# Four projection matmuls drawn in front of a class-side score step instead of between its matmuls

## The chip, the cores and the metric

The kernel runs on one core of one Trainium2 chip. The metric is the device time of one execution in microseconds. Before the change it is 1135.92 us, the median of three runs (1135.29 to 1136.38).

## What is computed

One decoder layer with 1024 positions and width 1024, in float32. The normalised input goes through one projection; a quarter of its width feeds a pooling mixer, three quarters feed twelve attention heads of 64 channels. Each head is evaluated under three windowed patterns, and the three results are merged by their softmax denominators. Then come the output projection and a gated feed-forward part, each with a norm and a residual.

```python
DILATED_CONFIGS = ((128, 1), (512, 4), (2048, 16))
...
def reference(x, ...):
    h = rms_norm(x, ln_pre_mix[l])
    proj = h @ w_in[l]
    q, k = rope(q, pos), rope(k, pos)
    pool_out = multi_scale_pool(u_pool, w_pool[l], pool_scale[l])
    attn_out = dilated_attention(q, k, v).reshape(B, S, ATTN_WIDTH)
    mix = jnp.concatenate([pool_out, attn_out], axis=-1) @ w_out[l]
    x = x + rms_norm(mix, ln_post_mix[l])
    h = rms_norm(x, ln_pre_ffn[l])
    f = (jax.nn.silu(h @ w_gate[l]) * (h @ w_up[l])) @ w_down[l]
    x = x + rms_norm(f, ln_post_ffn[l])
```

## The kernel before, in words

**Units.** The heads are worked on in six pairs, and the positions in two halves h of 512. A pair and a half make a unit, twelve in all (0 to 11; `units`). Units 0, 2, 4, 6, 8 and 9 have h = 0, the others h = 1. Each unit has scores, a merge of the softmax terms, weights, turns (transposes of the weighted scores) and products with v.

**The scores.** `scores` (L802) makes eight steps of a unit: two heads `hd`, two sides, two steps `jj` each. Side 1 is the class side: positions with the same remainder by 4 are taken together, which serves the two dilated patterns. Side 0 is the natural side, positions in a row. A step takes one bank of PSUM (tag `s`, two banks that are used in turn) and makes four matmuls in it, two query blocks j times two parts n of q (`qh` high and `ql` low, which together hold float32 precision). q is the stationary operand, loaded into TensorE ahead of its matmul, and k the moving one. At the class side a query block is `q[n][:, hd, j::4]` (L823), at the natural side a run of 128 columns. At h = 0 a class block has 128 moving columns, at h = 1 it has 256 (`narrow`). VectorE then reduces each block with its mask (L846) and ScalarE exponentiates it (L849).

**The list of projections.** The projections of later units run between the attention steps, as a list of small steps (`Fill`, L679). A step of `proj_half` (L702) is one matmul of 512 columns, a step of `v_rows` (L738) two matmuls of 256 columns, and a step of `pool_proj` (L1010) one of 256; at the end of the attention a list of output projections takes over, with 512 columns. `pull` (L697) runs the next step of the current list, or nothing if the list is at its end. A plan, sorted by written positions (`emit`, L1080), sets which step comes when; slots of the list (`by`, L693) run it up to a given step, so that a step that has been pulled already isn't run again.

**Waiting.** `await_` (L659) keeps a planned clock. It pulls from the list until the clock has come to the due time of what the next step needs, for a score step the release of its bank (`("s", 0)`), and then makes a number of further pulls from a table. A pull counts 0.235 us on this clock, and the matmuls of a score step 0.47 us.

**Order.** All matmuls and transposes are kept in program order on TensorE (`mm`, L346), so that the order of the Python calls is that of the engine. At the class side the loop over n pulls once ahead of each of the four score matmuls (L831 to L834). In the profile a matmul is TensorE's PE, its weight load PEld; the tiles are `ps_s` for scores, `ps_pj` for most projections, `ps_t` for turns and `ps_o` for products.

Of the kernel before, what the change touches and what calls it, by code (L numbers as in the profile page):

```python
# [335 lines left out]
def view(ap, offset, dims):  # L336

    return bass.AP(tensor=ap.tensor, offset=ap.offset + offset, ap=[list(ap.ap[0])] + [list(d) for d in dims])
# [3 lines left out]
def hybrid_block(ctx: ExitStack, tc: tile.TileContext, xT, w_in, w_v, w_pin, w_pool, w_out, w_gate, w_up, w_down,  # L342
# [3 lines left out]
    def mm(*a, **k):  # L346
        return tc.keep_in_program_order(nc.tensor.matmul(*a, **k))  # L347
# [9 lines left out]
    def did(key):  # L357
        seen[key] = seen.get(key, 0) + 1

    def need(key, n):  # L360
        assert seen.get(key, 0) >= n, (key, n, seen.get(key, 0))
# [8 lines left out]
    def bank(tag):  # L370
        return psum.tile([P, 512], F32, name="ps_" + tag, tag=tag)
# [254 lines left out]
    def by_class(ap):  # L626

        return ap.rearrange("p (c r) -> p r c", c=4)
# [30 lines left out]
    def await_(*keys, step=None):  # L659

        at = max([due.get(k, 0.0) for k in keys] or [0.0])
        more, n = G["x"].get(step, 0), 0
        while clock[0] < at + min(0, more) * 0.235 and n < G["fl"]:
            f = Fill.now
            if f is None or f.n >= len(f.steps):
                break
            pull()
            n += 1
        for n in range(more):
            pull()  # L670
# [26 lines left out]
    def pull():  # L697
        f = Fill.now
        if f is not None and f.n < len(f.steps):
            f.upto(f.n + 1)  # L700
# [98 lines left out]
    def narrow(side, h, j):  # L799
        return h == 0 and (side == 1 or j == 0)  # L800

    def scores(pr, h):  # L802

        un = pr.un[h] = Pair()
        un.sx = small.tile([P, 2, 2, 4, 2, 2], F32, name="sx", tag="sx", bufs=2)
        un.pp = {}

        def step(hd, side, jj):
            did(("s", pr.p, h))
            for i in range(h + 1):  # L810
                need(("k", pr.p, i), pr.p > 0)
            if jj == 0:
                un.pp[hd, side] = att.tile([P, 4, 256], F32, name="pp", tag="pp", bufs=PPB)
            pt = un.pp[hd, side]
            sx = un.sx
            q, kc = pr.q[h], pr.k
            await_(("s", 0), step=(unit_of[pr.p, h], "s", 4 * hd + 2 * (1 - side) + jj))
            s = bank("s")
            for j in (2 * jj, 2 * jj + 1):
                qb = 4 * h + j  # L820
                nb = 1 if narrow(side, h, j) else 2
                so = s[:, (j % 2) * 256:(j % 2) * 256 + nb * P]
                qs = slice(j * P, (j + 1) * P) if side == 0 else slice(j, 512, 4)  # L823
                kk = kc[:, hd]
                if side:
                    rhs = kk.rearrange("p (h c r) -> p h c r", h=2, c=4)[:, :nb, j]
                else:

                    b = qb + 1 - nb
                    rhs = view(kk, b // 4 * 512 + b % 4 * 32, [[P, 4]] + ([[32 + (b % 4 == 3) * 384, 2]] if nb == 2 else []) + [[1, 32]])  # L830
                for n in range(2):  # L831
                    if side:
                        pull()
                    mm(so, q[n][:, hd, qs], rhs, start=(n == 0), stop=(n == 1))  # L834
            clock[0] += 0.47
            due["s", 0], due["s", 1] = due.get(("s", 1), 0.0), clock[0] + G["ls"]
            due["m", pr.p, h] = clock[0] + G["lm"]
            for j in (2 * jj, 2 * jj + 1):
                nb = 1 if narrow(side, h, j) else 2
                lo = 256 - nb * P  # L840
                so = s[:, (j % 2) * 256:(j % 2) * 256 + nb * P]
                row, mask = pt[:, j, lo:], (mB if side else mA)[:, lo:]
                if side == 0:
                    so = by_class(so)
                    row, mask = (x.rearrange("p (r c) -> p r c", c=4) for x in (row, mask))
                nc.vector.tensor_tensor_reduce(  # L846
                    row, so, mask, op0=ALU.add, op1=ALU.min, scale=-0.125,
                    scalar=3e38, accum_out=sx[:, 0, side, j, hd, 0:1])
                nc.scalar.activation(pt[:, j, lo:], pt[:, j, lo:], AF.Exp,  # L849
                                     bias=sx[:, 0, side, j, hd, 0:1], scale=-1.0,  # L850
                                     accum_out=sx[:, 0, side, j, hd, 1:2])
        return [lambda a=a: step(*a) for a in [(hd, sd, jj) for hd in range(2) for sd in (1, 0) for jj in range(2)]]

    def merge(pr, h):
# [1114 lines left out]
```

## Time and profile before

| | us |
|---|---|
| median of three runs | 1135.92 |
| lowest and highest | 1135.29, 1136.38 |
| the profiled execution's own time | 1135.46 |
| its span on the core | 1133.6 |
| TensorE matmuls busy | 1125.0 |
| TensorE weight loads busy | 978.1 |
| VectorE busy | 782.1 |
| GpSimd busy | 587.1 |
| ScalarE busy | 563.8 |

The profile shows one execution. A row of the time line has the start in us from the beginning of the span, the duration in us, the engine, the line, the operation, the tiles (out<-in), the size of the array that is used, the shape (partitions x elements) and how many alike were merged (x1 is a single one). Matmuls are pipelined, so one starts before its predecessor's row has ended: the distance between the starts of two rows, not the duration, says what a matmul costs. A row of a group has the busy time in us, the mean in ns and, behind the bar, the idle time ahead. A row of waits has who waited for whom, the sum in us, the number of waits and the longest.

### The profile page before, as it was taken

The numbers are of one execution on the slowest core, as the hardware profiler recorded it, in microseconds if no ns is written. First come the engines' busy times: TensorE is split into PE (matmuls) and PEld (weight loads), VectorE is DVE, ScalarE is ACT, GpSimd is POOL, SyncE is SP. The second block draws the span as 40 slices with busy tenths as digits, with TensorE's granted clock in tenths as the row PEclk, the third lists the DMA queues.
The fourth block names the chain that finished last, engine by engine and source line by source line (L and its number), as shares of the span: only waits on it lengthen the run. The fifth ranks groups of instructions, "written<-read, shape, count | busy, mean of one in ns | idle before, by whom it ended". The sixth has DMA issues, their size and how long they took to land.

```text
span 1133.6 us, 17084 instructions
## 1 busy us (share of the span) xinstructions
PE 1125.0 (99%) x6076; PEld 978.1 (86%) x6076; DVE 782.1 (69%) x1455; ACT 563.8 (50%) x1092; POOL 587.1 (52%) x497
## 2 busy tenths in 40 slices
PE   9999999999999999999999999999999999999997
PEld 7999999999899888888788888888888888888897
DVE  7966879787987666979566755676566375464594
ACT  7356676776777765856323322322232436344430
POOL 0103645363576023242678655977586977665631
PEclk9999999999999999999999999999999999999999
DMA  8324151515137467430344344535454869766642
GB/s 285 118 80 168 57 168 41 183 57 167 58 112 263 168 221 276 151 112 28 140 167 176 148 158 160 204 139 204 168 185 168 278 207 369 247 198 195 204 167 75
DMA packets 85366, 189.04 MB, mean 167 GB/s; under 512 B 8736, under 2 KB 23584, under 8 KB 83872
## 3 DMA queue, kind: packets, MB, share of 16 engines
q1 hardware_dynamic: 84992, 187.68, 47.7%
q8 instruction: 48, 0.79, 0.3%
q14 instruction: 38, 0.31, 0.1%
q10 hardware_dynamic: 288, 0.27, 0.1%
HBM read 134.96 MB, written 52.95 MB: 166 GB/s over the span
## 4 chain that ended last, share of the span: by engine, by line
PE 93%; DMA 2%; POOL 2%; issue 1%; DVE 1%; SPq 0%; ACT 0%; DVEq 0%; POOLq 0%; ACTq 0%
PE ps_pj L347 34%; PE ps_s L347 24%; PE ps_o L347 23%; PE ps_t L347 8%; PE ps_t L350 3%; DMA wraw<-in_w_v_dram 1%; POOL whl L1561 1%; POOL fw L1561 1%; DMA rw<-in_w_up_dram 1%; DMA wraw<-in_w_in_dram 0%; DVE sq L510 0%; DMA ls<-in_lsel_dram 0%; PE ps_o L350 0%; POOL y L1762 0%; SPq L494 0%
## 5 line engine op out<-in xcount | busy, mean ns | idle before, releaser
L347 PE MATMUL ps_pj<-x,whl 128*128 128x512 f32 x480 | 141.8, 408 | 0.0
L1561 POOL TENSOR_TENSOR fw<-rw,fw 128x512 fp32r<-128x512 f32 x74 | 100.5, 1383 | 62.0 <-ACT fw L1559 62.0
L347 PE MATMUL ps_o<-tT,fw 128*128 128x512 f32 x504 | 117.8, 389 | 0.7 <-DVE p L1596 0.7
L907 POOL TENSOR_SCALAR pp<-pp,wv 128x256 f32<-128x256 f32 (+1 forms) x111 | 53.3, 502 | 115.8 <-ACT u L1025 45.6
L347 PEld LDWEIGHTS ps_o<-tT,fw 128*128 128x128 f32 x504 | 94.5, 188 | 20.7 <-DVE p L1596 1.1
L402 POOL TENSOR_TENSOR whl<-wraw,whl 128x512 fp32r<-128x512 f32 x52 | 68.9, 1347 | 73.8 <-ACT whl L398 71.8
L849 ACT ACTIVATE pp<-pp,sx 128x128 f32<-128x128 f32 (+1 forms) x192 | 89.4, 467 | 27.6 <-DVE sx L846 26.9
L1561 POOL TENSOR_TENSOR whl<-rw,whl 128x512 fp32r<-128x512 f32 x42 | 61.9, 1498 | 62.9 <-ACT whl L1559 62.9
L347 PEld LDWEIGHTS ps_pj<-x,whl 128*128 128x128 f32 x480 | 84.1, 189 | 9.1
L1559 ACT ACTIVATE fw<-rw 128x1024 fp32r<-128x1024 f32 x37 | 38.6, 1057 | 100.5 <-DVE rw L1527 45.2
L347 PE MATMUL ps_pj<-whl,x 128*128 128x256 f32 x528 | 81.4, 289 | 0.0
L1708 POOL TENSOR_TENSOR op<-rw,op 128x512 fp32r<-128x512 f32 x38 | 60.5, 1591 | 37.5 <-ACT op L1707 34.8
L1707 ACT ACTIVATE op<-rw 128x1024 fp32r<-128x1024 f32 x38 | 40.2, 1060 | 67.2 <-PE ps_t L347 32.7
L347 PEld LDWEIGHTS ps_pj<-whl,x 128*128 128x128 f32 x528 | 70.0, 192 | 0.2
L621 POOL TENSOR_TENSOR rsw<-rsw,sinr 128x512 f32<-128x512 f32 x20 | 26.8, 1339 | 81.3 <-DVE rsw L619 81.3
L955 DVE TENSOR_TENSOR ptr<-ps_t,ptr 128x512 fp32r<-128x512 f32 (+1 forms) x84 | 56.0, 667 | 17.8 <-ACT ptr L954 17.1
L954 ACT ACTIVATE ptr<-ps_t 128x512 fp32r<-128x512 f32 (+1 forms) x84 | 48.2, 574 | 28.7 <-PE ps_t L350 27.5
L347 PE MATMUL ps_pj<-b,fw 128*128 128x512 f32 x264 | 61.6, 389 | 0.0
L347 PEld LDWEIGHTS ps_pj<-b,fw 128*128 128x128 f32 x264 | 49.6, 188 | 10.3
L347 PE MATMUL ps_o<-ptr,v 128*128 128x128 f32 (+1 forms) x472 | 55.7, 254 | 0.0
L347 PEld LDWEIGHTS ps_o<-ptr,v 128*128 128x128 f32 x472 | 52.3, 163 | 3.2 <-DVE mix L921 0.3
L347 PE MATMUL ps_s<-k,qh 128*128 128x128 f32 (+1 forms) x192 | 54.4, 295 | 0.0
(322 smaller groups left out, 2921.5 us busy)
## 6 DMA issues: line engine op xcount, KB each, us to landing
rw<-bd SPq DMA_DIRECT2D x77, 256.0 KB, 4.9
v<-vd SPq DMA_DIRECT2D x22, 512.0 KB, 4.3
rw<-wsd SPq DMA_DIRECT2D x44, 256.0 KB, 4.0
rw<-in_w_gate_dram SPq DMA_DIRECT2D x20, 512.0 KB, 3.8
rw<-in_w_up_dram SPq DMA_DIRECT2D x20, 512.0 KB, 4.8
bd<-p SPq DMA_DIRECT2D x33, 256.0 KB, 2.7
rw<-in_w_down_dram SPq DMA_DIRECT2D x33, 256.0 KB, 4.7
fw<-in_w_down_dram SPq DMA_DIRECT2D x16, 512.0 KB, 4.0
```

The costliest lines, as they stand in the source:

```text
L347: return tc.keep_in_program_order(nc.tensor.matmul(*a, **k))
L350: return tc.keep_in_program_order(nc.tensor.transpose(dst, src, by))
L402: parts.append(eng.tensor_tensor(dst[:, 1, at:at + w], src[:, at:at + w], dst[:, 0, at:at + w].bitcast(F32), ALU.subtract))
L621: pin(eng[0].tensor_tensor(s, s, sinr[:, sl], ALU.mult))
L849: nc.scalar.activation(pt[:, j, lo:], pt[:, j, lo:], AF.Exp, bias=sx[:, 0, side, j, hd, 0:1], scale=-1.0, accum_out=sx[:, 0, side, j, hd, ...
L907: nc.gpsimd.tensor_scalar(pv, pv, un.wv[:, side, j, hd:hd + 1], 1.0, op0=ALU.mult, op1=ALU.mult)
L954: nc.scalar.activation(ptr[:, 0, :w], t[:, :w], AF.Copy)
L955: nc.vector.tensor_tensor(ptr[:, 1, :w], t[:, :w], ptr[:, 0, :w].bitcast(F32), ALU.subtract)
L1559: nc.scalar.activation(w[n][:, :, 0], raw[n], AF.Copy)
L1561: low[0] = nc.gpsimd.tensor_tensor(w[n][:, i, 1], raw[n][:, i], w[n][:, i, 0].bitcast(F32), ALU.subtract)
L1707: nc.scalar.activation(w[:, :, 0], raw, AF.Copy)
L1708: nc.gpsimd.tensor_tensor(w[:, 0, 1], raw[:, 0], w[:, 0, 0].bitcast(F32), ALU.subtract)
```

## The change

At the class side the step's four pulls are made at once, ahead of the step's `await_`. The pull ahead of each score matmul is gone, so that the four score matmuls are issued one after the other. At the natural side (side 0) `range(4 * side)` is empty, and nothing changes.

```diff
             sx = un.sx
             q, kc = pr.q[h], pr.k
+            for n in range(4 * side):
+                pull()
             await_(("s", 0), step=(unit_of[pr.p, h], "s", 4 * hd + 2 * (1 - side) + jj))
             s = bank("s")
             for j in (2 * jj, 2 * jj + 1):
...
                 for n in range(2):
-                    if side:
-                        pull()
                     mm(so, q[n][:, hd, qs], rhs, start=(n == 0), stop=(n == 1))
```

## The prediction

> **What bounds the kernel now.** I read the page first (busy shares, then the chain that ended last), then TensorE's own waits, then the groups of its weight loads, then the time line of TensorE around the steps that the diff touches.
>
> ```profile
> span 1133.6 us, 17084 instructions
> ...
> PE 1125.0 (99%) x6076; PEld 978.1 (86%) x6076; DVE 782.1 (69%) x1455; ACT 563.8 (50%) x1092; POOL 587.1 (52%) x497
> ```
>
> ```profile
> PE ps_o L347 <- DVE warm L454: 1.5, 1, 1.5
> PE ps_o L347 <- DVE p L1596: 0.7, 1, 0.7
> ```
>
> TensorE is busy 99% of the span, and the waits that it has on other engines add up to about 2 us, and both rows lie outside the attention units (the warm-up ahead of them, the feed-forward half behind). So there is no slack on TensorE into which longer work could go: what the score steps cost more or less on TensorE comes out at the end almost one to one. A busy 99% does not say that the stream runs at its best rate, though. A matmul has a weight load in front of it, and the question is which of the two sets the distance to the next matmul.
>
> ```profile
> L347 PEld LDWEIGHTS ps_pj<-x,whl 128*128 128x128 f32 x480 | 84.1, 189 | 9.1
> ...
> L347 PEld LDWEIGHTS ps_s<-k,ql 128*128 128x128 f32 x192 | 48.1, 251 | 1.1
> ```
>
> Both loads have the same shape, 128x128, but the load for a score takes 251 ns in the mean against 189 ns for one of a projection. Half of the score loads are class side. There q is read at every fourth column (`qs = slice(j, 512, 4)`, L823); the natural half reads it in a row. The class loads are the long ones, as the time line shows:
>
> ```profile
> 272.88 0.31 PEld L347 LDWEIGHTS ps_s<-k,ql 128*128 128x128 f32 x1
> 273.09 0.33 PEld L347 LDWEIGHTS ps_s<-k,qh 128*128 128x128 f32 x1
> 273.33 0.33 PEld L347 LDWEIGHTS ps_s<-k,ql 128*128 128x128 f32 x1
> ```
>
> They last 0.31 to 0.33 us and begin 0.21 and 0.24 us after one another.
>
> **The change, part by part.** The edit adds no instruction and takes none away. It moves four pulls (each one step of the running list of projection matmuls) from between the four class scores to the front of the step, ahead of its `await_`. No DMA is tied to the scores; a projection's first pull issues its weight DMA (SP) and split (ScalarE, GpSimd or VectorE), its last pull hands the result to the rope on VectorE, GpSimd and ScalarE; these now stand ahead of the step's score reductions and exponentials instead of between them. I cost that at nothing: it is less than one step earlier, and the busiest of these engines is at 69% (rival 3 is the case without that cover).
>
> *Interleaved, as it is now, 256 columns* (units with h = 1; unit 7's second class step):
>
> ```profile
> 275.54 0.40 PE L347 MATMUL ps_pj<-x,whl 128*128 128x512 f32 x1
> 275.77 0.28 PE L347 MATMUL ps_s<-k,qh 128*128 128x256 f32 x1
> ...
> 276.95 0.40 PE L347 MATMUL ps_pj<-x,whl 128*128 128x512 f32 x1
> ```
>
> The four pulls and four scores between the first and the last row take 276.95 - 275.54 = 1.41 us.
>
> *Following each other.* Unit 7's first class step had an exhausted list, so its four scores already stand together behind projections: exactly the new pattern.
>
> ```profile
> 272.64 0.40 PE L347 MATMUL ps_pj<-x,whl 128*128 128x512 f32 x1
> 272.88 0.28 PE L347 MATMUL ps_s<-k,qh 128*128 128x256 f32 x1
> ...
> 273.70 0.40 PE L347 MATMUL ps_pj<-x,whl 128*128 128x512 f32 x1
> ```
>
> From the last projection to the matmul after the scores 1.06 us pass. The other three pulls run at the plain distance of projections:
>
> ```profile
> 306.51 1.55 PE L347 MATMUL ps_pj<-x,whl 128*128 128x512 f32 x6
> 307.90 0.22 PE L347 MATMUL ps_s<-k,qh 128*128 128x128 f32 x1
> ```
>
> Six in 1.39 us, 0.232 each, so three take 0.70. New step: 0.70 + 1.06 = 1.76 us, **0.35 more** than 1.41. The reading: now each long load lies under a 512-column projection, afterwards only the first does, and the others set the distance.
>
> The Trainium skill ("TensorE: Matmul & The Clock Gate", section "LDWEIGHTS (loading the stationary operand)") speaks against this: it says that a load's time depends on the number of columns alone, about columns / 1.2 in ns, an estimated 107 ns for these 128. By it the class scores would follow each other as closely as natural ones, which is the first rival. The 251 against 189 ns at equal column count disagree.
>
> *128 columns* (h = 0), interleaved in unit 8:
>
> ```profile
> 307.66 0.40 PE L347 MATMUL ps_pj<-x,whl 128*128 128x512 f32 x1
> ...
> 309.00 0.29 PE L350 MATMUL ps_t<-pmt,pp 128*128 128x128 f32 x1
> ```
>
> That is 1.34 us. Three scores in a row after one 512-column pull stand in unit 4:
>
> ```profile
> 179.19 0.45 PE L347 MATMUL ps_pj<-x,whl 128*128 128x512 f32 x1
> 179.48 0.22 PE L347 MATMUL ps_s<-k,ql 128*128 128x128 f32 x1
> 179.54 0.40 PE L347 MATMUL ps_s<-k,qh 128*128 128x128 f32 x1
> 179.78 0.40 PE L347 MATMUL ps_s<-k,ql 128*128 128x128 f32 x1
> 180.01 0.30 PE L350 MATMUL ps_t<-idt,pp 128*128 128x128 f32 x1
> ```
>
> The second score comes 0.06 after the first (its load began before), the others 0.24 apart. Four: 0.70 for three pulls, 0.24 from the fourth to the first score (272.64 to 272.88), 0.53 for three scores, 0.24 for one more: 1.71 us, **0.37 more**.
>
> *Pulls of 256 columns.* A step of the v list pulls two matmuls of 256 columns, one of the pool list pulls one. Interleaved, from the first score to the matmul behind the last (v in unit 2, then pool in unit 0):
>
> ```profile
> 132.62 0.34 PE L347 MATMUL ps_s<-k,qh 128*128 128x128 f32 x1
> ...
> 134.18 0.30 PE L350 MATMUL ps_t<-pmt,pp 128*128 128x128 f32 x1
> ```
>
> ```profile
> 70.13 0.34 PE L347 MATMUL ps_s<-k,qh 128*128 128x128 f32 x1
> ...
> 71.33 0.33 PE L347 MATMUL ps_pj<-whl,x 128*128 128x256 f32 x1
> ```
>
> Together after 256-column matmuls (unit 9's first step, list exhausted):
>
> ```profile
> 326.89 0.53 PE L347 MATMUL ps_o<-ptr,v 128*64 128x256 f32 x3
> 327.25 0.34 PE L347 MATMUL ps_s<-k,qh 128*128 128x128 f32 x1
> ...
> 328.13 0.29 PE L350 MATMUL ps_t<-pmt,pp 128*128 128x128 f32 x1
> ```
>
> A 256-column matmul costs 0.36 / 3 = 0.12, the four scores 0.88. v: now 1.56, then 6 x 0.12 + 0.88 = 1.60; pool: now 1.20, then 3 x 0.12 + 0.88 = 1.24. The load is too long for a 256-column cover already, so little is lost: 0.03 for v, nothing for pool (its next matmul now comes late by as much).
>
> *How many.* I walked the time line through all 48 class steps (12 units, two heads, two each). Fully interleaved with 512-column pulls are 26, the first and the last beginning with
>
> ```profile
> 91.00 0.28 PE L347 MATMUL ps_s<-k,qh 128*128 128x256 f32 x1
> ```
>
> ```profile
> 396.05 0.40 PE L347 MATMUL ps_s<-k,qh 128*128 128x256 f32 x1
> ```
>
> 17 of them have 256 columns (4, 2, 4, 3, 4 in units 1, 3, 5, 7, 11), 9 have 128 (2, 2, 2, 3 in units 2, 4, 6, 8). Three are partly so (first of units 4, 6, 8, with 1, 2 and 2 pulls between scores), and unit 9's last is mixed (I count 1.5); a pull drawn out from between costs a third of 0.35 to 0.37, 0.12. Eight have v pulls, four pool pulls, unit 10's first has one pull; five have none (first of 7 and 9, three of unit 10).
>
> Sum: 17 x 0.35 = 5.95; 9 x 0.37 = 3.33; 6.5 x 0.12 = 0.8; 8 x 0.03 = 0.2: **+10.3 us**.
>
> *What the moved pulls do to the planner and the score bank.* `await_` pulls until the planned clock has reached the bank's due time. The four pulls now count before it looks, so it draws up to four fewer; those are drawn later by the plan's own slots, and TensorE does the same number. The score bank is asked for at least as late as now. A run of four class scores takes 0.8 to 0.9 us, while the planner books 0.47, so every later due time is met with more real time to spare. I cost this part at nothing; the cover is the pulls. Both ends: a pull left for each of the five bare steps would cover one load and save 0.1 each (-0.5), and an upset of waits elsewhere I allow 1 us, half of all TensorE waits above.
>
> The profiled execution took 1135.46 us, span 1133.6 plus 1.9 around it, and stands 0.46 below the median 1135.92. 1135.46 + 10.3 = 1145.8; on the median it is 1146.2. I say **1146.0**.
>
> **Rivals.**
>
> *1. The long load is hidden or a class run costs what a natural run costs: faster.* A natural run now:
>
> ```profile
> 278.32 0.28 PE L347 MATMUL ps_s<-k,qh 128*128 128x256 f32 x1
> ...
> 278.79 0.39 PE L347 MATMUL ps_pj<-x,whl 128*128 128x512 f32 x1
> ```
>
> Four in 0.47, 0.12 each. Then 512-pull steps take 0.70 + 0.24 + 0.47 = 1.41: nothing on 17, +0.07 on 9 (+0.6); v 0.72 + 0.47 = 1.19 instead of 1.56 (8 x -0.37 = -3.0); pool 0.36 + 0.47 = 0.83 instead of 1.20 (4 x -0.37 = -1.5). Sum -3.9: 1132 us. A hundredth of a microsecond per score is 38 x 4 x 0.01 = 1.5 us, so the sign turns at about 0.145 us per score in a run. For it: TensorE does begin loads early (the 0.06 above). Against it: in unit 4's rows the third score, and what follows it, come at 0.24.
>
> *2. The pulls don't meet the scores any more: no change, 1136.* If the list were mostly empty at class steps, nothing would move. Against it: 43 of 48 steps have a pull between their scores now.
>
> *3. The wait moves to VectorE and back: about 1153.*
>
> ```profile
> DVE pp L846 <- PE ps_s L347: 23.7, 37, 1.9
> ```
>
> VectorE already stands 37 times at the head of its queue for a score. The first pair of scores is now complete later in its step; what is queued behind that reduction (the low halves of the turned weights, the ropes' reads of a projection bank) frees banks that TensorE needs. If half of a step's growth, 0.18 us, came back as a TensorE wait in 38 steps, that adds 7. Against it: no attention wait on TensorE now, and VectorE is at 69%.
>
> **How the numbers follow.** Forecast 0.86, rival 1 0.03, rival 2 0.04, rival 3 0.07. Range: below, loads in a run at 0.21 (272.88 to 273.09 in the rows of the weight loads) instead of 0.235 save 0.025 x 3 x 26 = 2.0, and the planner's 1.5: 1142.5. Above, a second score that costs 0.235 too, 0.12 to 0.18 more in 26 steps, is 3 to 4.7: 1150.5. A measurement of this kernel can tell about 0.2% (2.3 us) from no change; slower by more than that 0.93, within it 0.04, faster 0.03.
>
> **What would show it.** In the new trace: class scores in fours at 0.24 us with loads of 0.33; the mean of the score loads up from 251 ns; natural steps as now; TensorE's waits still near 2 us; the attention units ending about 10 us later and everything after them of the same length. Wrong it would be if runs came at 0.12, if TensorE waited on VectorE, or if pulls still stood between class scores.

## The result and the profile after

The changed kernel takes 1144.55 us, the median of six runs (1144.02 to 1144.97), beside 1135.72 us (1135.29 to 1136.52) for the kernel before on the same chips: 8.8 us more, ratio 1.0078 with a 95% interval of 1.0068 to 1.0088. The forecast was 1146.0 us.

The page of the changed kernel, span and busy times:

```profile
span 1142.9 us, 17084 instructions
...
PE 1133.6 (99%) x6076; PEld 983.4 (86%) x6076; DVE 779.4 (68%) x1455; ACT 564.9 (49%) x1092; POOL 587.0 (51%) x497
```

The span is 9.3 us longer and TensorE is busy 8.6 us longer. The other engines do what they did. TensorE's waits on other engines, all of them:

```profile
PE ps_o L347 <- DVE warm L454: 1.5, 1, 1.5
PE ps_o L347 <- DVE p L1596: 0.9, 1, 0.9
PE ps_t L347 <- DVE turned L620: 0.5, 1, 0.5
PE ps_s L347 <- ACT x L501: 0.2, 1, 0.2
```

They come to 3.1 us; none belongs to a score step. So the time went into TensorE's own stream. Unit 7's second class step, whose old order the prediction showed with 1.41 us, in the time line after:

```profile
280.59 1.85 PE L347 MATMUL ps_pj<-x,whl 128*128 128x512 f32 x7
282.28 0.28 PE L347 MATMUL ps_s<-k,qh 128*128 128x256 f32 x1
282.40 0.39 PE L347 MATMUL ps_s<-k,ql 128*128 128x256 f32 x1
282.63 0.39 PE L347 MATMUL ps_s<-k,qh 128*128 128x256 f32 x1
282.86 0.39 PE L347 MATMUL ps_s<-k,ql 128*128 128x256 f32 x1
283.10 0.39 PE L347 MATMUL ps_pj<-x,whl 128*128 128x512 f32 x1
```

Seven projections run at 0.24 us, then come the four scores, and from the first of them to the next projection 0.82 us pass. The second score comes 0.12 after the first, the others and the projection behind them 0.23 to 0.24 apart. With 128 columns, in unit 6, only the second distance differs (0.06):

```profile
250.22 0.22 PE L347 MATMUL ps_s<-k,qh 128*128 128x128 f32 x1
250.28 0.40 PE L347 MATMUL ps_s<-k,ql 128*128 128x128 f32 x1
250.52 0.40 PE L347 MATMUL ps_s<-k,qh 128*128 128x128 f32 x1
250.76 0.40 PE L347 MATMUL ps_s<-k,ql 128*128 128x128 f32 x1
250.99 0.45 PE L347 MATMUL ps_pj<-x,whl 128*128 128x512 f32 x1
```

Twice the columns, and the same distance: the matmul does not set it. The weight loads of the 256-column step come at that distance too:

```profile
282.28 0.31 PEld L347 LDWEIGHTS ps_s<-k,ql 128*128 128x128 f32 x1
282.49 0.33 PEld L347 LDWEIGHTS ps_s<-k,qh 128*128 128x128 f32 x1
282.73 0.33 PEld L347 LDWEIGHTS ps_s<-k,ql 128*128 128x128 f32 x1
```

A load begins 0.21 to 0.24 us after the one before. At most one load is ahead: the second begins with the first score's matmul (282.28), not under the projections before it. So it is in both whole traces: none of the 6076 loads begins before the matmul ahead of its own has begun. The group of these loads after:

```profile
L347 PEld LDWEIGHTS ps_s<-k,ql 128*128 128x128 f32 x192 | 49.2, 256 | 1.2
```

Its mean rose only from 251 to 256 ns. What changed is not how long a load lasts but what lies over it.

**Where the 9.3 us are.** The last natural step of unit 11 began at 401.60 us before and begins at 410.69 after, 9.1 us later:

```profile
401.60 0.28 PE L347 MATMUL ps_s<-k,qh 128*128 128x256 f32 x1
```

```profile
410.69 0.28 PE L347 MATMUL ps_s<-k,qh 128*128 128x256 f32 x1
```

Nearly all of it has come by the end of the scores; what follows is as long as before but for 0.2 us. I measured each of the 48 class steps in both traces: from the start of the matmul ahead of the first score to the start of the one behind the last, less the plain distance of the pulls in between and of the matmul ahead (0.232 us for 512 columns, 0.118 for 256 and for the two transposes that stand ahead of a step). What remains is the cost of four scores:

| class steps, by their pulls before | steps | before, us | after, us | difference in sum, us |
|---|---|---|---|---|
| 512 columns, 256-column scores | 17 | 0.517 | 0.823 | 5.21 |
| 512 columns, 128-column scores | 9 | 0.430 | 0.765 | 3.02 |
| 512 columns in part (units 4, 6, 8, 9) | 4 | 0.597 | 0.768 | 0.69 |
| 256 columns (v, pool) | 13 | 0.871 | 0.890 | 0.25 |
| none | 5 | 0.903 | 0.902 | -0.01 |

The sum is 9.2 us, which accounts for the shift of 9.1.

### The profile page after: what moved, and what is told of

It reads as the page before. It is cut to its first block, busy times and chain, and to the rows that moved or that the text cites. A ratio compares the mean times of both kernels' runs of the same rounds, so it can differ in the third digit from the quotient of the medians.

```text
span 1142.9 us, 17084 instructions
## 1 busy us (share of the span) xinstructions
PE 1133.6 (99%) x6076; PEld 983.4 (86%) x6076; DVE 779.4 (68%) x1455; ACT 564.9 (49%) x1092; POOL 587.0 (51%) x497
## 4 chain that ended last, share of the span: by engine, by line
PE 93%; DMA 2%; POOL 2%; issue 1%; DVE 1%; SPq 0%; ACT 0%; DVEq 0%; POOLq 0%; ACTq 0%
PE ps_pj L347 34%; PE ps_s L347 25%; PE ps_o L347 23%; PE ps_t L347 8%; PE ps_t L350 3%; POOL whl L1561 1%; DMA wraw<-in_w_v_dram 1%; POOL fw L1561 1%; DMA rw<-in_w_up_dram 1%; DMA wraw<-in_w_in_dram 1%; DVE sq L510 0%; DMA ls<-in_lsel_dram 0%; PE ps_o L350 0%; POOL y L1762 0%; SPq L494 0%
## 5 line engine op out<-in xcount | busy, mean ns | idle before, releaser
L347 PE MATMUL ps_pj<-x,whl 128*128 128x512 f32 x480 | 134.1, 404 | 0.0
L347 PE MATMUL ps_pj<-whl,x 128*128 128x256 f32 x528 | 74.3, 287 | 0.0
L347 PEld LDWEIGHTS ps_pj<-whl,x 128*128 128x128 f32 x528 | 67.0, 191 | 0.2
L347 PE MATMUL ps_s<-k,ql 128*128 128x128 f32 (+1 forms) x192 | 63.3, 339 | 0.0
L347 PE MATMUL ps_s<-k,qh 128*128 128x128 f32 (+1 forms) x192 | 58.5, 317 | 0.0
L347 PEld LDWEIGHTS ps_pj<-b,fw 128*128 128x128 f32 x264 | 49.5, 188 | 10.3
```

## The experiments

Theory A is the prediction's: a class load reads q at every fourth column, takes 0.21 to 0.24 us in a row of such loads, and is free only under a 512-column matmul. Times stand beside the kernel before on the same chip.

**The pulls behind the wait.**

```diff
-            for n in range(4 * side):
-                pull()
             await_(("s", 0), step=(unit_of[pr.p, h], "s", 4 * hd + 2 * (1 - side) + jj))
+            for n in range(4 * side):
+                pull()
```

This diff is against the changed kernel; those below are against the kernel before, where nothing else is said.

> The four pulls stay together, but come behind the step's await_ instead of ahead of it, so the planner's clock looks before it has them, as in the kernel before. Theory A (the class loads of q, 0.21 to 0.24 us each, lie uncovered when the four scores follow each other): nothing changes against the changed kernel, 1144.6 us within 1. Theory B (the loss comes from the pulls standing ahead of await_, so that the planner draws other steps at other places): back to about 1136.

Measured 1144.69 us, ratio 1.0074 (1.0057 to 1.0091); the changed kernel has 1.0078. Where the pulls stand against `await_`, and what the planner makes of it, costs nothing that can be measured. Theory B falls.

**Two and two.**

```diff
+                for n in range(2 * side):
+                    pull()
                 for n in range(2):
-                    if side:
-                        pull()
                     mm(so, q[n][:, hd, qs], rhs, start=(n == 0), stop=(n == 1))
```

> Two pulls ahead of each block of queries, then its two scores: runs of two instead of four. Theory A: in a run of two one load of two is uncovered and the second score comes early (0.06 or 0.12 us behind the first), so a step costs at 256 columns 2 x (0.23 + 0.235 + 0.117 + 0.235) = 1.63 us against 1.41 interleaved, at 128 columns 2 x (0.23 + 0.235 + 0.06 + 0.235) = 1.52 against 1.34 to 1.38: 17 x 0.22 + 9 x 0.15 = about +5 us, 1141. Theory B: 1136, since await_ looks first. Theory C (any break of the alternation costs the whole): 1144.6.

Measured 1141.38 us against 1136.26, ratio 1.0046 (1.0032 to 1.0061): 5.1 us, as theory A has it, though within an interval of 3.6 to 6.9; in the trace of one execution the class steps give 5.9 by the table's method. Half of the loads keep their cover, and about 0.6 of the loss remains. Theory C falls.

**q read in a row, interleaved and in runs.** The two runs that take the suspected cost away, the first in the kernel before, the second in the changed kernel. Both leave out the reading by class, so their class scores are those of other queries, and their times only price the stride:

```diff
-                qs = slice(j * P, (j + 1) * P) if side == 0 else slice(j, 512, 4)
+                qs = slice(j * P, (j + 1) * P)
```

> Kernel before, but the class side reads its block of q in a row, as the natural side does, in place of every fourth column; so the class scores are those of other queries, with the same shapes and the same number of instructions. Theory A (the stride of q makes the load long): score loads at 188 ns, interleaved steps of 512 pulls and 256 columns as now (bound by the matmuls, 1.41), those of 128 columns 9 x -0.2 = -2, v and pool steps 12 x -0.37 = -4.4, the five bare steps -2: about 1127 us. Theory D (the length of the class load comes from something else, the moving k or the bank): 1135.7, unchanged.

> Changed kernel (four pulls in front, four scores together) with the class side reading its block of q in a row, as in the run before; the class scores are those of other queries. Theory A: a run of four costs what a natural run costs, 0.12 us a score, and the order is worth almost nothing: within 2 us of the interleaved kernel that reads in a row, about 1127. Theory D (the run itself costs, through the bank or the moving k): about 9 us above that kernel, or 1144.6 if the reading in a row changes nothing.

Measured 1128.16 us interleaved, ratio 0.9933 (0.9918 to 0.9947), and 1128.48 us in runs, 0.9933 (0.9918 to 0.9948). Reading in a row takes 8 us off the kernel before, and then the order is worth nothing that can be measured. The weight loads of the interleaved one:

```profile
L347 PEld LDWEIGHTS ps_s<-k,ql 128*128 128x128 f32 x192 | 36.4, 190 | 1.2
```

They last 190 ns in the mean, as the projections' do (189). And a class step of unit 7 in the kernel with runs:

```profile
277.01 0.40 PE L347 MATMUL ps_pj<-x,whl 128*128 128x512 f32 x1
277.24 0.28 PE L347 MATMUL ps_s<-k,qh 128*128 128x256 f32 x1
277.36 0.28 PE L347 MATMUL ps_s<-k,ql 128*128 128x256 f32 x1
277.47 0.28 PE L347 MATMUL ps_s<-k,qh 128*128 128x256 f32 x1
277.59 0.28 PE L347 MATMUL ps_s<-k,ql 128*128 128x256 f32 x1
277.71 0.63 PE L347 MATMUL ps_pj<-x,whl 128*128 128x512 f32 x2
```

0.12 us a score, in the same bank, with the same moving k and the same order of pulls as after the change. The only difference is q's stride, so theory D falls too. One part of my expectation was wrong: the nine 128-column steps with 512-column pulls were to give 2 us and give 0.1 (0.430 to 0.417 a step). Under a 512-column matmul the long load had cost next to nothing. The gain came from the steps without such cover: the ten v and pool steps with 128-column scores fell from 0.851 to 0.400 us each (4.5 us), the five bare ones from 0.903 to 0.514 (1.9 us), three v steps with 256-column scores gave 1.4 and the four with cover in part 0.8. So part of the agreement with the expected 1127 is luck: a term that was too large stood beside terms that were too small.

**One half alone.**

```diff
+            for n in range(4 * side * h):
+                pull()
...
-                    if side:
+                    if side and not h:
                         pull()
```

> The change in the units with h = 1 alone (range(4 * side * h) in front, pulls between the scores where h is 0). It splits the sum. The class steps of the changed kernel, each against its own step before, say that the 17 steps with 256 columns give 5.2 us and the h = 0 units the other 3.9. Expected by theory A with these sizes: +5.2, about 1141.2 us; by the prediction's own sizes (0.35 for each of 17): +6.0, 1142.0.

Measured 1140.51 us against 1135.64, ratio 1.0041 (1.0027 to 1.0055): 4.9 us. In its trace the 17 steps give 5.21 us by the table's method. Both sizes lie within the interval (1.0027 to 1.0055 is 3.1 to 6.2 us), so the time alone does not decide between them; the steps of the trace do.

**A copy of q by class.** With it the class side could read its own queries in a row. The kernel's on-chip memory is full: one 4 KB tile (`rb`) is free after the beginning, and the pool of q has room for 2 KB more. The first try gives the low part a tile of 64 rows a head, without the zeros that fill up the 128:

```diff
+        hc = con1.tile([P, 2, 512], F32R, name="qch", tag="rb", bufs=1)
+        lc = qkp.tile([P, 512], F32R, name="qcl", tag="qcl", bufs=1)
+        for a in range(2):
+            nc.scalar.activation(hc[:, a].rearrange("p (c r) -> p c r", c=4),
+                                 hi[:, a].bitcast(F32).rearrange("p (r c) -> p c r", c=4), AF.Copy)
...
+                        own = slice(64 * hd, 64 * hd + 64) if n else slice(0, P)
+                        qc = pr.qc[h][1][own] if n else pr.qc[h][0][:, hd]
+                        mm(so, qc[:, j * P:(j + 1) * P], rhs[own] if n else rhs, start=(n == 0), stop=(n == 1))
```

> Kernel before, interleaved, with a copy of q by class for every unit but unit 0: high part by two ScalarE copies into a tile that shares the place of rb, low part by two VectorE copies into a tile of 64 rows a head, so the low class matmul contracts over 64 rows. The class loads are then read in a row and the result is the layer's. Theory A: the gain of reading in a row (8.1 us in e3) less unit 0's four steps (4 x 0.37 = 1.5), about 1129.7 us if the copies lie beside TensorE's work; up to 1134 if they delay other work of ScalarE and VectorE. Rival: the copies come late and TensorE waits for them at each unit's first class score, 11 x 0.5 us or more: 1135 and above.

Measured 1164.66 us, ratio 1.0253 (1.0239 to 1.0267): far off, and not for the rival's reason. The copies come in time: TensorE's only wait for one is 0.2 us. (A version with the copies planned earlier, 0.35 instead of 0.2 of a unit ahead of the scores, gave no result.) A class step of unit 5:

```profile
222.52 0.28 PE L347 MATMUL ps_s<-k,qch 128*128 128x256 f32 x1
222.63 0.39 PE L347 MATMUL ps_pj<-x,whl 128*128 128x512 f32 x1
222.96 0.38 PE L347 MATMUL ps_s<-k,qcl 64*128 64x256 f32 x1
223.27 0.50 PE L347 MATMUL ps_pj<-x,whl 128*128 128x512 f32 x1
```

The high score, read in a row, costs 0.11. Around the low one, which uses 64 rows of the array, both distances grow: 0.33 from the projection to it and 0.31 from it to the next, against 0.24 and 0.12 for a long class score before. Its weight load, in the same place:

```profile
222.52 0.19 PEld L347 LDWEIGHTS ps_pj<-x,whl 128*128 128x128 f32 x1
222.96 0.18 PEld L347 LDWEIGHTS ps_s<-k,qcl 64*128 64x128 f32 x1 [0.25 <-issue]
223.26 0.19 PEld L347 LDWEIGHTS ps_pj<-x,whl 128*128 128x128 f32 x1
```

It does not begin until its matmul does (222.96), and the load behind it not until the next matmul (223.26): at a change between 64 and 128 rows no load went ahead, at none of the 88 low scores. The two distances around these scores sum to 20.3 us more than before, of 29.1 in the span. TensorE's waits grew from 2.4 to 6.4 us; the rest was not traced. The next runs go back to 128 rows.

In the first the low part stays strided:

```diff
+                    if side and h in pr.qc and n == 0:
+                        mm(so, pr.qc[h][:, hd, j * P:(j + 1) * P], rhs, start=True, stop=False)
```

In the second GpSimd copies it into a tile of 128 rows, which takes the place of a buffer of raw weights:

```diff
+            own = slice(64 * a, 64 * a + 64)
+            nc.gpsimd.tensor_copy(qclow[own, a].rearrange("p (c r) -> p c r", c=4),
+                                  lo[own, a].bitcast(F32).rearrange("p (r c) -> p c r", c=4))
...
-        r = own or wpool.tile([P, 1024], F32, name="wraw", tag="wraw", bufs=3)
+        r = own or wpool.tile([P, 1024], F32, name="wraw", tag="wraw", bufs=2)
```

In the third GpSimd copies the high part too (the diff is against the second):

```diff
-            nc.scalar.activation(hc[:, a].rearrange("p (c r) -> p c r", c=4),
-                                 hi[:, a].bitcast(F32).rearrange("p (r c) -> p c r", c=4), AF.Copy)
+            nc.gpsimd.tensor_copy(hc[:, a].rearrange("p (c r) -> p c r", c=4),
+                                  hi[:, a].bitcast(F32).rearrange("p (r c) -> p c r", c=4))
```

> Kernel before with a copy by class of q's high part alone (two ScalarE copies a unit, in the place of rb); the low part is read at every fourth column as before, and all class matmuls contract over 128 rows. Every second class load is then short. Theory A: the long load still needs cover, so half of what reading in a row gave in the units from 1 on (half of 6.5): about -3, 1132.8 us; if the copies delay other work as they may have in e6, up to 1137. Theory E (e6's loss comes from the copies and their places, not from its 64-row matmuls): 1150 or more.

> Copies by class of both parts of q: the high part on ScalarE in the place of rb, the low part on GpSimd into a tile of 128 rows with the zeros kept, with one buffer of raw weights fewer (two instead of three) to make room. No matmul over 64 rows. Theory A with free copies: -6.5, about 1129.5 us; with the weights late by the missing buffer or the copies in the way, up to 1137. Theory E: 1150 or more.

> As the run before, with the copy of the high part on GpSimd too, so that ScalarE has nothing added. If ScalarE's copies were in the way of the weighted scores' turns, faster than that run by 1 to 3 us; if GpSimd's order is (its weight splits and weighing stand behind the copies), slower.

Measured 1142.01 (ratio 1.0055, 1.0037 to 1.0073), 1160.55 (1.0212, 1.0196 to 1.0228) and 1161.34 us (1.0228, 1.0212 to 1.0244): all three missed the times of theory A. In the first the class scores did get cheaper (the distances around them sum to 3.7 us less than before), but TensorE now waits where it did not. Its longest wait in that kernel:

```profile
PE ps_s L347 <- DVE ex L876: 3.4, 3, 2.0
```

The merge's small matmuls wait three times for VectorE. What they wait for stands in the queues with the exponentials and the copies (22 of 1.13 us on ScalarE); that the copies themselves push it back, and not another order of the instructions on these engines, was not separated. Moving the high copies from ScalarE to GpSimd, in the third, did not help.

The clock fell as well. In the first kernel TensorE's waits come to 8.4 us (2.4 before), and 1.5 us behind the longest of them the granted clock was 0.51 for 3.4 us (379.9 to 383.3), where eight matmuls of 512 columns took 0.38 us each instead of 0.24. In the kernel before the clock falls only at the very end, from 1129.6 us on. In the second and the third it was at half for about 13.7 us each ahead of their last microseconds: an estimated 6.8 us of lost work, half of 13.7.

The second and the third land where theory E put them, at 1150 or more, yet that does not show theory E: they lose 13.2 and 12.9 us behind the last score, where the first try and the first of these, which keep three buffers of raw weights, lose 0.3 and 0.15. The missing weight buffer shows there in the second:

```profile
PE ps_s L347 <- POOL fw L402: 3.3, 1, 3.3
```

What these two lose inside the attention, 11.7 and 13.4 us, was not split further.

At last only the steps that lack cover, with the memory that there is (the second run has these copies on GpSimd):

```diff
+    COPIED = {2: (1,), 3: (0,), 4: (1,), 6: (1,), 9: (0, 1), 10: (0, 1)}
...
+        for a in COPIED[unit_of[pr.p, h]]:
+            nc.scalar.activation(hc[:, a].rearrange("p (c r) -> p c r", c=4), hi[:, a].bitcast(F32).rearrange("p (r c) -> p c r", c=4), AF.Copy)
```

> Kernel before with class copies only where its class steps lack a 512-column cover: units 2, 4 and 6 for the second head, 3 for the first, 9 and 10 for both; high part by ScalarE, low part by VectorE, the low part of the second head alone (2 KB, all the room there is). 8 high and 5 low copies instead of 22 and 22. Gain by the trace of before: 4 x 0.37 (units 2, 4, 6) + 0.4 (unit 3) + 0.95 (unit 9) + 1.2 (unit 10) = about -4 us, 1132 us, if so few copies delay nothing. Rival: a copy delays ScalarE's and VectorE's other work as in e8 (about +9 us there with 22 copies), in proportion +3: 1135.

> As the run before with these copies on GpSimd. If the delay comes from ScalarE's and VectorE's queues, 1132 us; if from GpSimd's own order, which weight splits and ropes pass through, above that run.

Measured 1136.31 us against 1135.44, ratio 1.0007 (0.9998 to 1.0016), and 1136.04, ratio 1.0004 (0.9995 to 1.0013): no difference from the kernel before on either engine, where 1132 was expected. Class scores give back 4.8 us in the first one's trace. Merges, turns and products take 4.6, and natural scores and the time ahead of the first unit 1.7. No version here that computes the class scores of the right queries beats the kernel before.

## Why the prediction was right, point by point

- **TensorE has no slack, so its longer work shows at the end.** Right: 9.2 us more in the class steps, 9.3 in the span, and waits that grew by 0.7 us in all (2.4 before, with one of 0.2 beside the two rows shown, and 3.1 after).
- **A run costs 0.24 us a score but for the second.** Right, for both widths, in all 26 steps that had been covered; the bare steps of the old trace were the new pattern.
- **0.35 for each of 17 steps with 256 columns: 5.95.** Mis-sized; they give 5.21. The run's price was right. The price before was taken from one interleaved step, and five of the 17 had been dearer than it. Unit 11's second step before:

```profile
384.76 0.51 PE L347 MATMUL ps_s<-k,qh 128*128 128x256 f32 x1
...
386.17 0.38 PE L350 MATMUL ps_t<-pmt,pp 128*128 128x128 f32 x2
```

  1.41 us from the first score to the matmul behind the last, where unit 7's step had 1.18 (275.77 to 276.95). So this step had little left to lose.
- **0.37 for each of 9 steps with 128 columns: 3.33.** The same: 3.02, since three of the nine cost 0.06 to 0.08 more than unit 8's before.
- **Steps in part 0.8, v 0.2, pool nothing.** 0.69 for the first, 0.25 for v and pool together: right.
- **The planner and the bank cost nothing.** Right: the first experiment moved the pulls behind `await_` and found the same time.
- **The sum.** 10.3 forecast, 9.2 in the steps, 8.8 in the medians. Nearly all of the 1.1 us between forecast and steps lies in the 17 and the 9 (0.74 and 0.31).

Of the rivals, the first (a run costs what a natural run costs) names the condition rightly: with q read in a row it is what happened. The Trainium skill's rule, that a weight load depends on its columns alone ("TensorE: Matmul & The Clock Gate", section "LDWEIGHTS (loading the stationary operand)"), holds among the loads of 128 columns that matmuls behind the warm-up read in a row, 188 to 193 ns in the mean of each group in this kernel, though not with the 107 ns that are estimated from it. The loads of as many columns at every fourth one have 0.31 to 0.33 us, so here the measurement decides against it. The Trainium skill ("SBUF — State Buffer", section "Specifications (TRN2)", the row on cachelines) says that the on-chip memory has lines of 16 bytes and that each access that crosses to a new one pays. Every fourth float32 is exactly a new line for each column; the runs fit that, but none varied the stride to show that it is the reason. The second and third rivals did not come: the four pulls had met the scores nearly everywhere, and no attention wait on VectorE appeared.

## What to carry to other kernels

Where TensorE is full, the order of matmuls matters through the weight loads: only one load goes ahead, so a long load needs a long matmul right in front of it, and alternating long matmuls with long loads hides what grouping lays bare. Look for loads of one shape with different durations, and price a new order from a place where the old trace happens to have it already; but take the price of the old order as a mean over all its places, not from the one that is easiest to read. And a cost that is found is not yet a gain: taking the stride away is worth 8 us in a kernel that computes other scores, and the copies that it needs gave all of it back.

## What the runs showed of the hardware that was not expected

- The stationary operand at every fourth float32 column: loads of 0.31 to 0.33 us instead of 0.19, beginning 0.21 to 0.24 us apart. Under a 512-column matmul the difference is almost free (0.430 against 0.417 us for four scores of 128 columns).
- A matmul over 64 rows with 256 moving columns, between 512-column matmuls over 128 rows: 0.32 us ahead of it and 0.31 behind in the mean of 24, with neither its load nor the next one begun early. Less work in the array cost more time than the zeros that it left out.
- The granted clock fell to half for 3.4 or 6.8 us at a time in the middle of a kernel, once in the first of the three kernels with 128-row copies, three times in the second and four in the third. Each time it fell during a wait of TensorE of 1.0 to 3.8 us or within 2 us behind it, but not at every such wait; what sets it off was not tested.
